# Splitting weight tiles into high and low halves: by ScalarE and GpSimd before, by two GpSimd-queue transfers after

## The chip, the cores and the metric

The kernel runs on one core of one Trainium2 chip. The metric is the device time of one execution in microseconds (us). Engines are named as the profile names them: PE is TensorE (PEld its weight loads), DVE is VectorE, ACT is ScalarE, POOL is GpSimd, SP is SyncE, which issues transfers.

## What is computed

One layer of a hybrid decoder (512 tokens, width 1024) and a final RMSNorm: a sparse-attention branch and a state-space (SSD) branch read one normalised input, are merged by gates and projected, and a gated feed-forward block with a short convolution follows.

```python
h = rmsnorm(x, norm_mix)
(q, c_raw, q_idx, k_idx, w_idx, z, xbc, dt_raw, g_att, g_ssm) = split_cols(h @ w_in, IN_SPLITS)
att = dsa_attention(...)                      # 16 heads, each query keeps 128 keys
y = gated_group_rmsnorm(ssd_scan(conv(xbc)) + d_skip * xs, z, ssm_norm)
merged = sigmoid(g_att) * (att @ w_att_out) + sigmoid(g_ssm) * (y @ w_ssm_out)
x = x + merged @ w_out
u = causal_depthwise_conv(rmsnorm(x, norm_ffn) @ w_ffn_up, conv_ffn_w, conv_ffn_b)
gate, val = split(u)
x = x + (silu(gate) * val) @ w_ffn_down
return rmsnorm(x, norm_final)
```

All of it is float32. TensorE multiplies here in a rounded form of float32 (`fp32r`), so every operand is kept as two tiles: `hi`, the value rounded, and `lo`, what the rounding left over. A product is the sum of three matmul passes, hi by hi, hi by lo and lo by hi (`mm3`).

## The kernel before

Weights come from HBM in tiles of 128 partitions by 1024 float32 (512 KB): 168 by `weight()` and two more (`load_kv`). Each goes through four steps in the kernel before: SP issues the load of `wr` (raw, 2 buffers, L95); ACT copies it with rounding to `wh` (3 buffers, `split`, L86); POOL subtracts, `wl = wr - wh` (3 buffers, L87); PE uses both, 24 matmuls of 512 columns a tile in most places. A tile's buffer comes free when its last reader is done.

The stages stand in this order: the first norm, the key indexer (`pqidx`), the SSD mixer (four groups; projections `pxbc`, `pz` and `pso` on PE woven into the scan; L331 to L333 pick the top keys), attention (`pq`, `pgs`, softmax on DVE and ACT, the bias tiles `bm` on POOL), the merge (`pga` with wG and `pao` with wAO, one tile each in turn), the output projection (`pwo`), the up projection (`pup`, 44 tiles of wUp, L105) and the down projection (`pdn`, 22 tiles of wDn, L947). In the mixer POOL has two small jobs for each chunk: the state `Hs` (L563, 8 of them) and the chunk's output `y` (L551, 12 of them). DVE works there on the decay tiles `dec` (L524, L527) and on the split of `X` (L508). A scheduler (the tile framework's) sets the order on every engine, and each engine takes its instructions strictly in that order: one that waits holds up all behind it.

Of the kernel before, what the change touches and what calls it, by code (L numbers as in the profile page):

```python
# [14 lines left out]
P = 128  # L15
# [33 lines left out]
def _body(ctx, tc, x, prm_d, cst_d, nfin_d, wI_d, wX_d, wSO_d, wQ_d, wG_d, wAO_d, wO_d, wUp_d, wDn_d,  # L49
# [34 lines left out]
    def split(hi, lo, src, lo_eng=None):  # L84
        """hi = fp32r(src), lo = fp32r(src - hi)."""
        nc.scalar.activation(hi, src, AF.Copy)  # L86
        (lo_eng or nc.vector).tensor_tensor(lo, src, f(hi), OP.subtract)  # L87

    wcnt = [0]

    def weight(src, w=1024):
        i = wcnt[0]
        wcnt[0] += 1
        raw = wp.tile([P, w], F32, tag="wr", name=f"wr{i}", bufs=2)
        nc.sync.dma_start(raw, src)  # L95
        hi = wp.tile([P, w], R32, tag="wh", name=f"wh{i}", bufs=3)
        lo = wp.tile([P, w], R32, tag="wl", name=f"wl{i}", bufs=3)
        split(hi, lo, raw, lo_eng=nc.gpsimd)
        return hi, lo

    def mm3(ps, terms):
        """ps = sum of lhs.T @ rhs over terms of ((lhs_hi, lhs_lo), (rhs_hi, rhs_lo))."""
        seq = [(a[0], b[0]) for a, b in terms] + [(a[0], b[1]) for a, b in terms] + [(a[1], b[0]) for a, b in terms]
        for i, (l, r) in enumerate(seq):
            nc.tensor.matmul(ps, l, r, start=(i == 0), stop=(i == len(seq) - 1))  # L105

    def rsqrt(dst, ss, scale, eps, n, pool):
        """dst = (ss*scale + eps)^-0.5"""
        t = pool.tile([P, n], F32, tag="rsq", name="rsq")
        nc.vector.tensor_scalar(t, ss, scale, eps, OP.mult, OP.add)  # L110
        nc.gpsimd.tensor_tensor(dst, t, mhalf[:, :n], OP.pow)
# [7 lines left out]
    def norm_T(xts, gname, dst, pool, sq, scl):  # L119
        """dst = rmsnorm(xts).T in hi and lo; sq and scl: the engine (ACT or DVE) of each block's squares and scaling."""  # L120
        for hf in range(2):
# [32 lines left out]

# [1 line left out]
    mid_stack = ExitStack()  # L156
# [18 lines left out]
    with tc.tile_pool(name="n1", bufs=2) as n1:  # L175
# [17 lines left out]

# [1 line left out]
        ps = mmt("pkidx")  # L195
# [37 lines left out]

# [1 line left out]
        dx = dtS.rearrange("p a b -> p (a b)")  # L235
# [39 lines left out]

# [1 line left out]
        pu = cht("pu")  # L277
# [4 lines left out]

# [1 line left out]
    nc.vector.tensor_copy(msk[:, 0:P], cv("maskc"))  # L284
# [3 lines left out]
    def dup_q(ps, name, tags, pool, scale, bufs):  # L288
        """Per head of a pair, its rows hi and lo on both halves of the partitions."""
        out = []  # L290
        for hh in range(2):
            r, o = slice(64 * hh, 64 * hh + 64), slice(64 - 64 * hh, 128 - 64 * hh)
            hi = pool.tile([P, S], R32, tag=tags[2 * hh], name=f"{name}h{hh}", bufs=bufs)
            lo = pool.tile([P, S], R32, tag=tags[2 * hh + 1], name=f"{name}l{hh}", bufs=bufs)
            nc.scalar.activation(hi[r], ps[r], AF.Copy, scale=scale)
            nc.vector.scalar_tensor_tensor(lo[r], ps[r], scale, f(hi[r]), OP.mult, OP.subtract)
            nc.sync.dma_start(f(hi[o]), f(hi[r]))
            nc.sync.dma_start(f(lo[o]), f(lo[r]))
            out.append((hi, lo))
        return out  # L300
# [39 lines left out]

# [1 line left out]
    def weave(chain, fill):  # L342
        """Emit the chain's (weight, step)s in order, the fillers spread between them by weight."""
        total = sum(w for w, _ in chain) or 1
# [11 lines left out]
    def proj_steps(name, wsrc, after, parts=2):  # L356
        """One column tile of a projection of actT, in emission steps."""
        st = {}
# [291 lines left out]

# [1 line left out]
    attT = []  # L652
# [11 lines left out]
    def load_kv():  # L664
        for i, nm in enumerate(("uk", "uv")):
            raw = wp.tile([P, 1024], F32, tag="wr", name="wr" + nm, bufs=2)
            nc.sync.dma_start(raw, wkv_d[i])
            hi = ap_.tile([P, 1024], R32, tag=nm + "h", name=nm + "h", bufs=1)
            lo = ap_.tile([P, 1024], R32, tag=nm + "l", name=nm + "l", bufs=1)
            split(hi, lo, raw, lo_eng=nc.gpsimd)  # L670
            wkv.append((hi, lo))
# [113 lines left out]
    def pav_(h):  # L785
        """Even heads: [Vh|Vl], odd heads: [Vl|Vh], so that the low part lands on the other half of the partitions."""
        p, hh = h // 2, h % 2
# [69 lines left out]

# [1 line left out]
    at.close()  # L859
# [19 lines left out]

# [1 line left out]
    x1 = [big.tile([P, D], F32, tag=f"ys{b}", name=f"x1{b}") for b in range(NB)]  # L881
# [124 lines left out]
def _coltile(w):  # L1006
    """(K, N) -> (N/128, 128, K/128 * 128): per column tile, rows on partitions."""
    k, n = w.shape
# [77 lines left out]
```

## Time and profile before

| | us |
|---|---|
| median of 3 runs | 1191.85 (1189.85 to 1192.34) |
| span of the profiled execution | 1188.0 |
| PE busy | 1113.1 (94%) |
| DVE busy | 705.9 (59%) |
| ACT busy | 582.3 (49%) |
| POOL busy | 518.0 (44%), of which L87 `wl`: 409.8 |

The profiled execution's time outside its span is not listed; the median of the runs lies 3.85 us above the span, and that is taken for it (its time is then 1191.85 us, the median itself). The page's part 1 gives the busy times, part 4 the chain that ended last: PE 57%, DVE 26%, ACT 5%, issue 3%, POOL 2%, DMA 2%.

### The profile page before, as it was taken

The page shows a single profiled execution, that of the slowest core. Times are in us where ns is not written, and L with a number is a line of the kernel's source. Part 1 is how long each engine was busy: PE and PEld are TensorE (multiplying, and loading weights), DVE is VectorE, ACT ScalarE, POOL GpSimd, SP SyncE. Part 2 cuts the span into 40 slices and gives each one's busy share as a digit, 9 for nine tenths or more (in the row PEclk, how much of TensorE's full clock was granted, in tenths as well). Part 3 has the DMA queues.
Part 4 walks back from the last instruction along what each step waited for, and adds up shares of the span by engine and source line. Part 5 has one row for each costly group of instructions (what it writes and reads, how often), then busy time and mean ns, then how long its engine had stood idle before and what let it go on. Part 6 is the DMA issues. An engine that isn't in the chain of part 4 may idle for free.

```text
span 1188.0 us, 14616 instructions
## 1 busy us (share of the span) xinstructions
PE 1113.1 (94%) x5268; PEld 920.8 (78%) x5268; DVE 705.9 (59%) x1324; ACT 582.3 (49%) x942; POOL 518.0 (44%) x287
## 2 busy tenths in 40 slices
PE   5898996998999889899999899999999999999997
PEld 5677775876887678778878788888888888888885
DVE  5569999998579689368988833305533344330004
ACT  5356464557476555456667633215444444432113
POOL 3324343334524434566566444444444444444442
PEclk9989999999999899999999999999999999999999
DMA  5264322222322231443434133232332222222221
GB/s 186 90 184 143 107 81 80 89 87 74 116 80 83 86 116 59 122 127 107 129 102 125 47 110 123 107 110 86 106 106 90 104 91 99 97 89 107 89 105 73
DMA packets 43306, 122.06 MB, mean 103 GB/s; under 512 B 5393, under 2 KB 9761, under 8 KB 43233
## 3 DMA queue, kind: packets, MB, share of 16 engines
q1 hardware_dynamic: 42656, 120.07, 30.5%
q8 instruction: 42, 0.69, 0.2%
q10 hardware_dynamic: 576, 1.05, 0.2%
q14 instruction: 32, 0.25, 0.1%
HBM read 108.29 MB, written 5.32 MB: 96 GB/s over the span
## 4 chain that ended last, share of the span: by engine, by line
PE 57%; DVE 26%; ACT 5%; issue 3%; POOL 2%; DMA 2%; POOLq 0%; DVEq 0%; ACTq 0%
PE pup L105 20%; PE pdn L947 10%; PE pso L464 5%; PE pao L105 4%; PE pga L105 4%; PE pwo L891 3%; DVE dec L524 3%; DVE u L388 3%; PE pxbc L373 3%; DVE msk L333 2%; DVE dec L527 2%; DVE m L332 2%; DVE pr L747 1%; DVE pr L759 1%; DVE Ml L87 1%
## 5 line engine op out<-in xcount | busy, mean ns | idle before, releaser
L87 POOL TENSOR_TENSOR wl<-wr,wh 128x1024 fp32r<-128x1024 f32 x168 | 409.8, 2440 | 481.4 <-ACT wh L86 260.6
L86 ACT ACTIVATE wh<-wr 128x1024 fp32r<-128x1024 f32 x168 | 177.4, 1057 | 189.1 <-PE pdn L947 80.6
L930 DVE SCALAR_TENSOR_TENSOR fu<-pup,prm,fu 128x511 f32<-128x511 f32 x88 | 65.9, 749 | 124.2 <-ACT fu L928 122.6
L105 PE MATMUL pup<-hTh,wh 128*128 128x512 f32 (+1 forms) x368 | 88.0, 381 | 1.6 <-ACT hTh L144 0.8
L105 PE MATMUL pup<-hTl,wh 128*128 128x512 f32 (+1 forms) x368 | 87.7, 380 | 0.0
L105 PE MATMUL pup<-hTh,wl 128*128 128x512 f32 (+1 forms) x368 | 87.5, 380 | 0.0
L105 PEld LDWEIGHTS pup<-hTh,wh 128*128 128x128 f32 x368 | 67.2, 188 | 15.1 <-ACT hTh L144 1.1
L105 PEld LDWEIGHTS pup<-hTl,wh 128*128 128x128 f32 x368 | 67.2, 188 | 13.1
L105 PEld LDWEIGHTS pup<-hTh,wl 128*128 128x128 f32 x368 | 67.2, 188 | 13.1
L947 PE MATMUL pdn<-wl,fh 128*128 128x512 f32 x176 | 68.6, 390 | 1.2 <-POOL wl L87 1.2
L947 PE MATMUL pdn<-wh,fl 128*128 128x512 f32 x176 | 68.5, 389 | 0.0
L947 PE MATMUL pdn<-wh,fh 128*128 128x512 f32 x176 | 68.4, 390 | 0.0
L974 DVE TENSOR_TENSOR x<-pdn,x 128x512 f32<-128x512 f32 x8 | 5.5, 690 | 104.6 <-PE pdn L947 104.6
L439 PE MATMUL pz<-wh,hTh 128*128 128x512 f32 x128 | 52.4, 409 | 9.9 <-DVE u L388 9.9
L388 DVE SCALAR_TENSOR_TENSOR u<-pxbc,prm,u 128x511 f32<-128x511 f32 (+2 forms) x72 | 53.2, 739 | 9.7 <-ACT u L386 9.3
L373 PE MATMUL pxbc<-hTh,wh 128*128 128x512 f32 x192 | 53.8, 413 | 4.1 <-ACT wh L86 2.9
L524 DVE TENSOR_SCALAR dec<-dec,acS 128x128 f32<-128x128 f32 x128 | 50.6, 450 | 8.9 <-DMA dec<-acD 8.9
L373 PE MATMUL pxbc<-hTh,wl 128*128 128x512 f32 x192 | 51.1, 393 | 0.0
L440 PE MATMUL pz<-wl,hTh 128*128 128x512 f32 x128 | 50.9, 398 | 0.0
L441 PE MATMUL pz<-wh,hTl 128*128 128x512 f32 x128 | 50.9, 398 | 0.0
L373 PE MATMUL pxbc<-hTl,wh 128*128 128x512 f32 x192 | 50.0, 391 | 0.0
L464 PE MATMUL pso<-yTh,wh 128*128 128x512 f32 x128 | 38.7, 426 | 11.4 <-ACT wh L86 7.9
(360 smaller groups left out, 2554.2 us busy)
## 6 DMA issues: line engine op xcount, KB each, us to landing
wr<-wUp SPq DMA_DIRECT2D x44, 512.0 KB, 3.4
wr<-wX SPq DMA_DIRECT2D x40, 512.0 KB, 3.5
wr<-wDn SPq DMA_DIRECT2D x22, 512.0 KB, 3.5
dec<-acD SPq DMA_DIRECT2D x32, 256.0 KB, 3.3
wr<-wSO SPq DMA_DIRECT2D x16, 512.0 KB, 3.5
wr<-wG SPq DMA_DIRECT2D x16, 512.0 KB, 3.6
x<-x SPq DMA_DIRECT2D x8, 512.0 KB, 4.9
wr<-wQ SPq DMA_DIRECT2D x8, 512.0 KB, 3.5
```

Source lines behind the costliest of these rows:

```text
L86: nc.scalar.activation(hi, src, AF.Copy)
L87: (lo_eng or nc.vector).tensor_tensor(lo, src, f(hi), OP.subtract)
L105: nc.tensor.matmul(ps, l, r, start=(i == 0), stop=(i == len(seq) - 1))
L373: nc.tensor.matmul(st["ps"], *st["it"][i], start=(i == 0), stop=(i == 23))
L388: nc.vector.scalar_tensor_tensor(u[:, d:], ps[:, :S - d], pv("cw", o + 3 - d, o + 4 - d), u[:, d:], OP.mult, OP.add)
L439: nc.tensor.matmul(ps, actT[k][0][:, bs], wh[:, ws], start=(k == 0), stop=False)
L440: nc.tensor.matmul(ps, actT[k][0][:, bs], wl[:, ws], start=False, stop=False)
L441: nc.tensor.matmul(ps, actT[k][1][:, bs], wh[:, ws], start=False, stop=(k == KD - 1))
L464: nc.tensor.matmul(ps, *seq[i], start=(i == 0), stop=(i == 11))
L524: nc.vector.tensor_scalar(dec[:, r, :], dec[:, r, :], acS[:, c, r0 + r:r0 + r + 1], 0.0, OP.subtract, OP.min)
L930: nc.vector.scalar_tensor_tensor(u[:, d:], ps[:, :S - d], pv("fw", o + 2 - d, o + 3 - d), u[:, d:], OP.mult, OP.add)
L947: nc.tensor.matmul(po8[b][hf], l[:, bs], r[:, ws], start=(k == 0 and i == 0), stop=(k == NF - 1 and i == 2))
```

## The change

`weight()` and `load_kv` no longer load a raw tile. `wsplit` issues a transfer from HBM straight into the `fp32r` tile `wh` on POOL's queue (the transfer converts), ACT writes `-wh` into `wl`, and a second transfer on POOL's queue reads the same weights from HBM again and adds them onto `wl`. The raw buffers are gone; `wh` and `wl` have 4 buffers each instead of 3. The matmuls are the same. (The diff also drops comments, which are left out here; lines after L86 move by some.)

```diff
+    def wsplit(hi, lo, src):
+        nc.gpsimd.dma_start(hi, src)
+        nc.scalar.activation(lo, f(hi), AF.Copy, scale=-1.0)
+        nc.gpsimd.dma_start(lo, src, accum_op=OP.add)
+
     def weight(src, w=1024):
         i = wcnt[0]
         wcnt[0] += 1
-        raw = wp.tile([P, w], F32, tag="wr", name=f"wr{i}", bufs=2)
-        nc.sync.dma_start(raw, src)
-        hi = wp.tile([P, w], R32, tag="wh", name=f"wh{i}", bufs=3)
-        lo = wp.tile([P, w], R32, tag="wl", name=f"wl{i}", bufs=3)
-        split(hi, lo, raw, lo_eng=nc.gpsimd)
+        hi = wp.tile([P, w], R32, tag="wh", name=f"wh{i}", bufs=4)
+        lo = wp.tile([P, w], R32, tag="wl", name=f"wl{i}", bufs=4)
+        wsplit(hi, lo, src)
         return hi, lo
@@ load_kv
-            raw = wp.tile([P, 1024], F32, tag="wr", name="wr" + nm, bufs=2)
-            nc.sync.dma_start(raw, wkv_d[i])
...
-            split(hi, lo, raw, lo_eng=nc.gpsimd)
+            wsplit(hi, lo, wkv_d[i])
```

POOL in the up projection, tiles 119 to 121 of wUp, the kernel before (`wr` raw, `wh` high, `wl` low; in brackets the semaphores it waits for):

```order
L87 TENSOR_TENSOR wl119_8034<-wr119_8031,wh119_8033 128x1024 [waits DMAHW0_49,PE_49,Activation_49]
L87 TENSOR_TENSOR wl120_8076<-wr120_8073,wh120_8075 128x1024 [waits DMAHW1_49,PE_49,Activation_49]
L87 TENSOR_TENSOR wl121_8110<-wr121_8107,wh121_8109 128x1024 [waits DMAHW2_49,PE_49,Activation_49]
```

The same place after, tiles 119 to 122:

```order
L93 DMA wh119_7910<-wUp 128x1024 [waits PE_49]
L95 DMA wl119_7911<-wUp 128x1024 [waits DMASW3_49,PE_49,Activation_49]
L93 DMA wh120_7951<-wUp 128x1024 [waits DMASW4_49,PE_49]
L93 DMA wh121_7984<-wUp 128x1024 [waits DMASW6_49,DMASW5_49,PE_49]
L95 DMA wl120_7952<-wUp 128x1024 [waits Activation_49]
L95 DMA wl121_7985<-wUp 128x1024 [waits DMASW0_49,DMASW7_49,PE_49,Activation_49]
L93 DMA wh122_8025<-wUp 128x1024 [waits PE_49]
L95 DMA wl122_8026<-wUp 128x1024 [waits DMASW1_49,PE_49,Activation_49]
```

One subtraction a tile has become two transfers, in a pattern of three tiles that repeats: one tile's pair alone, then two high transfers followed by their two low ones; each low one waits for ACT's negation of its own high tile.

POOL in the merge, tiles 88 to 91 (wG and wAO in turn), after:

```order
L93 DMA wh88_6665<-wG 128x1024 [waits PE_49]
L93 DMA wh89_6697<-wAO 128x1024 [waits DMASW6_49,DMASW5_49,PE_49]
L95 DMA wl88_6666<-wG 128x1024 [waits Activation_49]
L95 DMA wl89_6698<-wAO 128x1024 [waits DMASW7_49,Activation_49]
L93 DMA wh90_6733<-wG 128x1024 [waits DMASW0_49,PE_49]
L93 DMA wh91_6765<-wAO 128x1024 [waits DMASW1_49,PE_49]
```

Here the transfers go by pairs of tiles, with no lone tile between.

POOL in the mixer's second group, around the first states and outputs (`Hs1`, `y1_1`; `wr`, `wh`, `wl` are weight tiles), before:

```order
L563 TENSOR_TENSOR Hs1_2120<-Hs1_2120,cdec_113 128x512 [waits DVE_49]
L87 TENSOR_TENSOR wl29_2270<-wr29_2267,wh29_2269 128x1024 [waits DMAHW4_49,PE_49,Pool_49]
L551 TENSOR_TENSOR y1_1_2151<-y1_1_2151,t11_1_2240 128x512 [waits DVE_49]
L87 TENSOR_TENSOR wl30_2299<-wr30_2296,wh30_2298 128x1024 [waits DMAHW6_49,PE_49,Activation_49]
L87 TENSOR_TENSOR wl31_2422<-wr31_2419,wh31_2421 128x1024 [waits DMAHW1_49,PE_49,Activation_49]
L563 TENSOR_TENSOR Hs1_2120<-Hs1_2120,cdec_113 128x512 [waits DVE_49]
```

The same place after:

```order
L567 TENSOR_TENSOR Hs1_2092<-Hs1_2092,cdec_113 128x512 [waits DVE_49]
L95 DMA wl30_2267<-wX 128x1024 [waits DMASW5_49,PE_49,Activation_49]
L93 DMA wh31_2388<-wX 128x1024 [waits DMASW6_49,PE_49]
L555 TENSOR_TENSOR y1_1_2123<-y1_1_2123,t11_1_2211 128x512 [waits DVE_49,Pool_49]
L93 DMA wh32_2419<-wSO 128x1024 [waits DMASW7_49,DMASW0_49,PE_49]
L95 DMA wl31_2389<-wX 128x1024 [waits Activation_49]
L95 DMA wl32_2420<-wSO 128x1024 [waits DMASW1_49,DMASW2_49,PE_49,Activation_49]
L567 TENSOR_TENSOR Hs1_2092<-Hs1_2092,cdec_113 128x512 [waits DVE_49]
```

Where one subtraction stood between the state and `y1_1`, two transfers stand now, and three where two subtractions stood; each waits for a landing, for PE or for ACT.

## Rows read from the trace of the kernel before

**Rows 1.** The table by stretches: busy time and count per engine, clock, DMA.
```profile
core 0: us, PE busy (x) PEld busy (x) DVE busy (x) ACT busy (x) POOL busy (x), PEclk, DMA share, GB/s
...
80.00:480.00 400.00, 367.42 (x1753) 301.62 (x1752) 350.18 (x673) 234.99 (x351) 155.82 (x74) 0.96 0.28 95
...
530.00:680.00 150.00, 143.31 (x773) 120.71 (x772) 129.50 (x304) 102.02 (x242) 92.78 (x82) 0.99 0.36 102
680.00:821.00 141.00, 138.87 (x628) 113.54 (x627) 46.79 (x56) 45.15 (x63) 62.08 (x29) 1.00 0.31 110
821.00:1060.00 239.00, 239.00 (x1095) 199.53 (x1094) 99.23 (x136) 109.66 (x139) 103.86 (x44) 1.00 0.28 97
1060.00:1188.00 128.00, 119.76 (x527) 98.32 (x525) 14.84 (x28) 29.95 (x41) 49.81 (x24) 0.98 0.25 91
```

**Rows 2.** The chain that ended last, its tail: start us, length us, what.
```profile
758.54 5.46 PE pga L105 x24
764.00 5.60 PE pao L105 x24
...
820.94 238.70 PE pup L105 x1092
1059.65 103.37 PE pdn L947 x456
```

**Rows 3.** The timeline of one up-projection weight: start, length, engine, idle before.
```profile
890.84 1.98 PE L105 MATMUL pup<-hTh,wh 128*128 128x512 f32 x8
...
891.14 2.42 POOL L87 TENSOR_TENSOR wl<-wr,wh 128x1024 fp32r<-128x1024 f32 x1 [3.03 <-PE pup L105]
...
894.72 1.06 ACT L86 ACTIVATE wh<-wr 128x1024 fp32r<-128x1024 f32 x1 [0.60 <-PE pup L105]
...
896.28 1.98 PE L105 MATMUL pup<-hTh,wh 128*128 128x512 f32 x8
```

**Rows 4.** The timeline of the first norm, VectorE beside GpSimd.
```profile
14.45 0.75 DVE L137 TENSOR_SCALAR xngmix<-x,nrsgmix 128x1024 f32<-128x1024 f32 x1 [0.66 <-POOL nrsgmix L111]
...
15.86 2.34 POOL L87 TENSOR_TENSOR wl<-wr,wh 128x1024 fp32r<-128x1024 f32 x1
15.93 2.82 DVE L137 TENSOR_SCALAR xngmix<-x,nrsgmix 128x1024 f32<-128x1024 f32 x1 [0.67 <-POOL nrsgmix L111]
```

**Rows 5.** VectorE groups of the mixer: count | busy us, mean ns | idle before.
```profile
L524 DVE TENSOR_SCALAR dec<-dec,acS 128x128 f32<-128x128 f32 x128 | 50.6, 450 | 8.9 <-DMA dec<-acD 8.9
...
L527 DVE TENSOR_TENSOR dec<-dec,cb 128x512 f32<-128x512 f32 x32 | 27.5, 880 | 5.6 <-ACT dec L526 5.6
...
L508 DVE TENSOR_TENSOR X<-xdt,X 128x256 fp32r<-128x256 f32 x32 | 20.5, 674 | 0.0
```

**Rows 6.** The same lines by tile: min/median/max ns.
```profile
L524 DVE TENSOR_SCALAR dec<-dec,acS x128: 262/277/2501, 98.8 to 444.9; 128x128 f32<-128x128 f32 x128
L527 DVE TENSOR_TENSOR dec<-dec,cb x32: 669/681/2337, 128.1 to 447.9; 128x512 f32<-128x512 f32 x32
...
L508 DVE TENSOR_TENSOR X<-xdt,X x32: 401/416/2614, 131.7 to 470.0; 128x256 fp32r<-128x256 f32 x32
```

**Rows 7.** The page, part 6: a weight load, KB, us from issue to landing.
```profile
wr<-wUp SPq DMA_DIRECT2D x44, 512.0 KB, 3.4
```

**Rows 8.** The timeline, one issue on SP.
```profile
0.74 0.38 SPq L181 DMA_DIRECT2D x<-x  x1
```

**Rows 9.** Waits of GpSimd in the mixer: us in total, times, longest.
```profile
POOL Hs L563 <- DVE Hl L87: 35.6, 8, 10.5
POOL y L551 <- DVE t L550: 32.0, 7, 7.0
```

## The prediction

> **What bounds the kernel now.** I read the table by stretches first, then the chain, then one weight tile in the timeline. The table [rows 1] shows two kinds of stretch. From 680 us on PE is the bound: it is busy for 138.87 of 141 us, 239.00 of 239 and 119.76 of 128, and the chain [rows 2] is PE alone, 238.70 us of up projection and 103.37 us of down projection almost in one piece. The timeline [rows 3] shows why POOL does not matter there: the same step of the next tile begins on PE at 896.28 after 890.84, so a tile lasts 5.44 us, and in that time ACT spends 1.06 us and POOL 2.42 us on splitting one tile, both waiting for PE. In the merge two tiles take 5.46 and 5.60 us [rows 2], 11.06 a pair. In the mixer (80 to 480 us) PE is busy for 367.42 of 400 us and DVE for 350.18 [rows 1]: both are near full, and they wait for each other. Attention (530 to 680) is alike: PE 143.31 of 150, DVE 129.50.
>
> **What the change removes.** 168 subtractions on POOL and the two of `load_kv`, 2.4 us each [rows 3]. In the PE-bound stretches that is worth nothing. In the mixer it is worth something by way of DVE. The same DVE instruction, L137 on 128x1024, takes 0.75 us alone and 2.82 us when it starts 0.07 us after a POOL subtraction [rows 4]: it stands still until POOL is done. The mixer has the same pattern: L524 has a median of 277 ns, a maximum of 2501 and a mean of 450 [rows 5, 6]. Busy time over count times median gives what the stalls cost: L524 50.6 - 128 x 0.277 = 15.1 us; L527 27.5 - 32 x 0.681 = 5.7; L508 20.5 - 32 x 0.416 = 7.2; together 28.0 us. As PE's idle time in this stretch is 32.6 us, the most that can be won is about that; I take 22, three quarters of the stall, since PE has work of its own for 367 us and what DVE gives back then meets it. SP loses 170 loads and the waits before them; what that frees is the decay tiles' load, for which DVE waited 8.9 us [rows 5], and this too lies within PE's 32.6. ACT does one copy a tile as before, 1.06 us: nothing.
>
> **What it adds: the price of a tile.** Per tile there are two transfers where there was one. Between 821 and 1060 us the transfers are nearly all weights, and they moved 97 GB/s at a share of 0.28 of the 16 DMA engines [rows 1], so 346 GB/s when all are at work, and 512 KB take 1.5 us. The high transfer is at least this copy: h = 1.5, no less; if the conversion halves the rate, 3.0; I take 1.5, the row of the same bytes from the same place. The accumulating transfer has to read the tile that it adds to besides the source. No row shows one. Its ends are 1.5 us (the second read is hidden) and 4.5 (two reads and a write one after the other); I take two reads, l = 3.0. It cannot be below zero, since the single load that both replace was hidden. The Trainium skill prices this in "Collectives: The Full Stack", section "The bandwidth ceiling": an add in the DMA engine costs its second read and nothing else, 62.28 GB/s for a copy against 32.35 for a reduction; by that estimate l would be 2.9 and the sum some 7 us lower. No run here shows it.
>
> **The cycle in POOL's queue.** POOL takes its queue in order, and in the up and down projections it repeats every three tiles: a high and its low transfer, then two high and their two low. A low one cannot be issued before its high one has landed and ACT has negated it, and everything behind waits with it; all of it goes through one queue, so a later transfer's bytes come behind the earlier ones. Landing takes 3.4 us from issue [rows 7], of which 1.5 is moving and about 0.4 the issue (SP's own takes 0.38 [rows 8]): 1.5 us from the last byte to the signal. Then ACT, 1.1, and the issue of the low transfer. What an issue costs on POOL no row shows: 0.38 us as on SP [rows 8], up to the 2.42 of the subtraction that it replaces [rows 3]; I take 0.5, near the row that is also an issue. So the DMA engines stand idle for 1.5 + 1.1 + 0.5 = 3.1 us behind the lone high transfer, and 3.1 - 1.5 = 1.6 us behind the pair, whose second transfer fills part of it. A cycle of three tiles takes 3 x (1.5 + 3.0) + 3.1 + 1.6 = 18.2 us. PE needs 3 x 5.44 = 16.3. PE, which never waited for weights here, then waits 1.9 us in every cycle. With 44 tiles of up and 22 of down projection, 22 cycles: **+42 us**. The fourth buffer covers the first few tiles; I leave that to the range. The point where it turns is h + l = (16.3 - 4.7) / 3 = 3.9 us a tile. The skill's "DMA: Bandwidth & Descriptors", section "Specifications", gives about 1 us to the first byte on GpSimd's path against 0.6 on SP's; by that estimate each cycle would lose 0.8 us more and the sum would be 18 us higher. No run here shows that either.
>
> **The other stretches.** In the merge the order is by pairs, 2 x 4.5 + 1.6 = 10.6 us against PE's 11.06: 0, with +30 at l = 4.5 (13.6 us, 12 pairs). In the mixer there are 51 tiles in 400 us, 7.8 us each, so the queue has room on average, but the 8 `Hs` and 12 `y` jobs of POOL now stand behind transfers that wait for a round trip of 3.4 + 1.1 + 0.5 = 5.0 us. Their cover is that POOL waits for their operands now, 35.6 and 32.0 us [rows 9], 3.4 us a job. What is left over, 1.6 us on 20 jobs, is 32 us if every job is hit and 0 if none; I take a third, +10, because DVE's next steps wait for these jobs. The mixer's net is -12. In attention the `bm` tiles on POOL lose as much to the same queue as DVE gains from fewer stalls: 0, between -7 (PE's idle time there) and +7.
>
> **The sum.** The profiled execution's time is its span of 1188.0 and the 3.85 around it, 1191.85, which is the median. 1191.85 - 12 + 42 = **1222 us**.
>
> **Rival one: the transfers keep up.** If h + l is under 3.9 us, say l = 1.5, a cycle takes 13.7 us, PE stays the bound from 680 us on, and the kernel keeps the 22 us of the mixer and some 5 of attention: 1165 us, at best 1152 with all of PE's idle time in both. For it speaks that DMA engines are at 0.28 to 0.36 in most stretches [rows 1]; against it, that a share does not tell the wait of a queue that goes in order.
>
> **Rival two: the transfers are slow.** With l = 4.5 a cycle takes 22.7 us: 22 x 6.4 = +141, the merge +30, and the mixer, at 7.6 us a tile against 7.8, loses its gain and the 10 us: 1191.85 + 181 = 1373 us. A conversion at half rate does the same. For it speaks that nothing in the trace adds or converts in a transfer, and that each microsecond on a tile costs 66 in the last two stages alone; against it, that plain bytes move at 346 GB/s.
>
> If the converting transfer did not round and only copied, the low half would be nothing but the same two transfers would run: no other time.
>
> **Chances.** Forecast case (h + l of 4 to 5.3 us, 1190 to 1300 us): 0.42. Rival one: 0.30. Rival two: 0.28. A measurement of this kernel tells about 0.2% from no change, 1189.5 to 1194.2 us; 0.03 falls there from the edges of the first two cases, so faster 0.29, slower 0.68. Of rival one a third lies below 1150, of rival two a third above 1400; so the range is 1150 to 1400. The forecast's own range is 1190 to 1300.
>
> **What would show it.** Between 821 us and the end PE should have gaps that end with a low tile's landing, one a cycle, and the up projection's piece of the chain should be near 270 us for 238.70. DVE's L524 should fall from 450 to below 300 ns a piece, and the time from 80 us to the query projections should be shorter by some 10 us. A low transfer should take about twice the engine time of a high one. The forecast is wrong if the up projection stays at 239 us (rival one), or goes beyond 300 (rival two).

## The result, and the profile after

The changed kernel takes **1286.14 us** (median; 1276.61 to 1291.41) against 1190.85 for the kernel before (1187.06 to 1192.34): ratio 1.0809, 95% interval 1.0751 to 1.0868. The profiled execution is the shortest of its runs, 1276.61 us with a span of 1274.8, so 1.8 us lie around the span. (It is 1.7 to 2.1 us in the runs of every kernel, so the profiled execution of the kernel before is the one of 1189.85 us, and the 3.85 taken ahead of the prediction is some 2 us too much.) The runs of the changed kernel differ by TensorE's granted clock: 0.966 of full speed in the shortest, 0.952 to 0.954 in those of 1291.3 and 1291.4.

To see where the time went, I cut both traces at the same events: the first matmul of `pxbc` (mixer), `pq` (attention), `pga` (merge), `pup` and `pdn`.

| stretch, us | before | after | measured | forecast |
|---|---|---|---|---|
| start | 76.1 | 79.0 | +2.9 | 0 |
| mixer | 402.7 | 402.1 | -0.6 | -12 |
| attention | 200.4 | 208.0 | +7.6 | 0 |
| merge, output projection | 137.3 | 150.9 | +13.6 | 0 |
| up projection | 243.0 | 270.6 | +27.6 | +28 |
| down projection, end | 128.5 | 164.3 | +35.8 | +14 |
| span | 1188.0 | 1274.8 | +86.8 | +30 |

(The forecast's +42 for both projections is divided by tiles, 44 and 22.)

The page of the changed kernel, parts 1, 3, 4 and 6: busy time, the queue that carries the weights, the chain that ended last, and issues (KB, median us from issue to landing).

```profile
PE 1134.6 (89%) x5268; PEld 927.3 (73%) x5268; DVE 617.0 (48%) x1324; ACT 572.5 (45%) x942; POOL 348.7 (27%) x457
...
q0 software_dynamic: 48960, 178.28, 61.0%
...
PE 31%; issue 23%; DMA 20%; DVE 11%; ACT 8%; POOL 6%; POOLq 0%; ACTq 0%; DVEq 0%; SPq 0%
DMA wh<-wUp 6%; PE pao L109 4%; PE pga L109 3%; DMA dec<-acD 3%; PE pup L109 3%; DMA wh<-wDn 3%; ACT wl L94 3%; PE pso L468 3%; PE pxbc L377 3%; POOL wh L93 3%; POOL wl L95 2%; PE pq L377 2%; DVE u L392 2%; DMA wh<-wX 2%; PE pwo L893 2%
...
wh<-wUp POOLq DMA_DIRECT2D x44, 512.0 KB, 6.8
...
dec<-acD SPq DMA_DIRECT2D x32, 256.0 KB, 5.6
```

PE was 57% of the chain and is 31% now; transfers and issue, 5% together before, are 43%. Of PE, DVE, ACT and POOL none is busier than it was, apart from PE by two percent (its clock, below): this is time spent waiting.

The same five stretches in the table by stretches (mixer, attention, merge, up, down), to hold against [rows 1], and behind them the first 60 us of the up projection alone:

```profile
core 0: us, PE busy (x) PEld busy (x) DVE busy (x) ACT busy (x) POOL busy (x), PEclk, DMA share, GB/s
79.00:481.00 402.00, 369.05 (x1768) 302.83 (x1767) 303.56 (x678) 238.34 (x358) 103.52 (x126) 0.97 0.69 161
481.00:689.00 208.00, 190.12 (x976) 159.01 (x976) 136.12 (x347) 123.12 (x275) 99.59 (x123) 0.97 0.72 166
689.00:840.00 151.00, 140.66 (x620) 113.71 (x618) 32.08 (x54) 43.24 (x62) 36.70 (x52) 0.99 0.75 179
840.00:1110.00 270.00, 249.71 (x1102) 203.75 (x1103) 94.84 (x136) 99.41 (x136) 60.55 (x86) 0.97 0.70 164
1110.00:1274.00 164.00, 131.86 (x532) 103.53 (x530) 17.18 (x32) 33.62 (x46) 30.94 (x44) 0.93 0.62 150
...
840.00:900.00 60.00, 60.00 (x310) 51.67 (x311) 23.36 (x37) 25.23 (x38) 13.59 (x20) 1.00 0.73 166
```

In the up projection PE was busy for all of 239.00 us; now it stands still for 20.3 of 270, and its 1102 matmuls take 249.71 us where 1095 took 239.00: the clock is 0.97 instead of 1.00. In the down projection idle time rises from 8.2 to 32.1 us and the same work from 119.76 to 131.86 us, at 0.93. The timeline of PE shows where the lower clock begins (start, length, what, idle time before):

```profile
986.17 3.62 PE L109 MATMUL pup<-hTh,wl 128*128 128x512 f32 x8 [2.61 <-DMA wl<-wUp]
...
1024.34 2.11 PE L109 MATMUL pup<-hTh,wl 128*128 128x512 f32 x8 [2.63 <-DMA wl<-wUp]
```

Eight matmuls take 1.98 us [rows 3]. Behind a wait of 2.61 us they take 3.62, nearly the double: most of them ran at the lower of the clock's two levels, 1.2 GHz for 2.4 (the granted clock is 0.57 from 986 to 990 us). Behind another wait of 2.63 us they take 2.11 (1.00 from 1024 to 1028). Of the ten waits for low tiles in this stage four, of 2.04 to 2.71 us, are followed by 3.1 to 3.6 us, and six, of 0.75 to 2.63, by 2.1. So the clock falls behind some of these waits and not behind others that are as long; what decides it, no run shows.

POOL's queue in the up and the down projection of the changed kernel (L93 high, L95 low):

```profile
964.00 0.88 POOL L93 DMA_DIRECT2D wh<-wUp  x1
972.08 0.85 POOL L95 DMA_DIRECT2D wl<-wUp  x1 [7.20 <-ACT wl L94]
972.62 1.42 POOL L93 DMA_DIRECT2D wh<-wUp  x2
980.62 0.88 POOL L95 DMA_DIRECT2D wl<-wUp  x1 [6.58 <-ACT wl L94]
982.23 0.87 POOL L95 DMA_DIRECT2D wl<-wUp  x1 [0.74 <-ACT wl L94]
982.78 0.88 POOL L93 DMA_DIRECT2D wh<-wUp  x1
...
1118.60 0.88 POOL L93 DMA_DIRECT2D wh<-wDn  x1
1126.53 0.85 POOL L95 DMA_DIRECT2D wl<-wDn  x1 [7.05 <-ACT wl L94]
1127.07 0.87 POOL L93 DMA_DIRECT2D wh<-wDn  x1
```

Read it by what stands between two high transfers. In the up projection a lone tile lasts from 964.00 to 972.62, 8.6 us, for 5.44 of PE's [rows 3]; a pair from 972.62 to 982.78, 10.2 us, for 10.9 of PE's. The whole cycle of three is 18.8 us. So a pair keeps up and a lone tile does not. This is one cycle; the twelve between 869.01 and 1099.06 us take 19.2 on average, a lone tile 8.2 to 9.3 us and a pair 9.8 to 11.2. In the down projection three lone tiles follow each other, the first of them shown: 8.5, 8.3 and 8.2 us. Over the whole stage a lone tile takes 8.1 to 10.7 us.

What POOL's transfers wait for in the up projection (860 to 1080 us), and the high ones of the down projection (1110 to 1260): us in total, times, longest.

```profile
POOL wl L95 <- ACT wl L94: 168.3, 34, 7.9
POOL wh L93 <- PE pup L109: 2.2, 1, 2.2
...
POOL wh L93 <- PE pdn L949: 0.6, 1, 0.6
```

The high transfers hardly ever wait for PE: the queue sets the pace, and PE follows it. The time that PE loses to its lower clock therefore comes, for the most part, out of time in which it would otherwise wait.

In the mixer most of the DVE stalls are gone and the stretch is no shorter. The group L528 of DVE there (count | busy, mean ns | idle before), which was L524 in [rows 5]:

```profile
L528 DVE TENSOR_SCALAR dec<-dec,acS 128x128 f32<-128x128 f32 x128 | 32.5, 311 | 32.4 <-DMA dec<-acD 32.3
```

The mean fell from 450 to 311 ns, DVE's busy time in the mixer from 350 to 304 us; but the wait for the decay tiles' loads rose from 8.9 to 32.3 us. ACT's and DVE's timelines show a second new wait:

```profile
318.14 1.06 ACT L94 ACTIVATE wl<-wh 128x1024 fp32r<-128x1024 f32 x1 [5.39 <-DMA wh<-wX]
319.11 1.13 ACT L86 ACTIVATE Mh<-dec 128x512 fp32r<-128x512 f32 x2
320.15 0.71 ACT L511 ACTIVATE X<-xdt 128x256 fp32r<-128x256 f32 x2
...
320.58 0.76 DVE L512 TENSOR_TENSOR X<-xdt,X 128x256 fp32r<-128x256 f32 x2 [4.88 <-ACT X L511]
```

ACT stands 5.39 us before the negation until a high tile has landed; `Mh` and `X` are queued behind it and go at once when it is done, and DVE has waited 4.88 us for that `X`.

### The profile page after: what moved, and what is told of

It reads as the page before. It is cut to its first block, busy times and chain, and to the rows that moved or that the text cites. A ratio compares the mean times of both kernels' runs of the same rounds, so it can differ in the third digit from the quotient of the medians.

```text
span 1274.8 us, 14670 instructions
## 1 busy us (share of the span) xinstructions
PE 1134.6 (89%) x5268; PEld 927.3 (73%) x5268; DVE 617.0 (48%) x1324; ACT 572.5 (45%) x942; POOL 348.7 (27%) x457
## 4 chain that ended last, share of the span: by engine, by line
PE 31%; issue 23%; DMA 20%; DVE 11%; ACT 8%; POOL 6%; POOLq 0%; ACTq 0%; DVEq 0%; SPq 0%
DMA wh<-wUp 6%; PE pao L109 4%; PE pga L109 3%; DMA dec<-acD 3%; PE pup L109 3%; DMA wh<-wDn 3%; ACT wl L94 3%; PE pso L468 3%; PE pxbc L377 3%; POOL wh L93 3%; POOL wl L95 2%; PE pq L377 2%; DVE u L392 2%; DMA wh<-wX 2%; PE pwo L893 2%
## 5 line engine op out<-in xcount | busy, mean ns | idle before, releaser
L94 ACT ACTIVATE wl<-wh 128x1024 fp32r<-128x1024 f32 x168 | 177.3, 1057 | 459.6 <-DMA wh<-wUp 139.3
L109 PE MATMUL pup<-hTh,wl 128*128 128x512 f32 (+1 forms) x368 | 94.3, 401 | 20.1 <-DMA wl<-wUp 20.1
L109 PEld LDWEIGHTS pup<-hTh,wl 128*128 128x128 f32 x368 | 69.5, 197 | 38.8 <-DMA wl<-wUp 25.3
L95 POOL DMA_DIRECT2D wl<-wUp x44 | 38.2, 868 | 209.8 <-ACT wl L94 205.1
L949 PE MATMUL pdn<-wl,fh 128*128 128x512 f32 x176 | 72.8, 414 | 20.6 <-DMA wl<-wDn 20.6
L95 POOL DMA_DIRECT2D wl<-wX x40 | 35.7, 893 | 189.2 <-ACT wl L94 175.4
L949 PE MATMUL pdn<-wh,fh 128*128 128x512 f32 x176 | 71.5, 409 | 3.7 <-DVE fu L932 3.6
L949 PE MATMUL pdn<-wh,fl 128*128 128x512 f32 x176 | 71.3, 405 | 0.0
L949 PEld LDWEIGHTS pdn<-wl,fh 128*128 128x128 f32 x176 | 34.7, 197 | 32.7 <-DMA wl<-wDn 25.5
L87 DVE TENSOR_TENSOR fl<-fu,fh 128x512 fp32r<-128x512 f32 x22 | 15.2, 692 | 78.1 <-ACT fh L86 78.1
L95 POOL DMA_DIRECT2D wl<-wDn x22 | 19.0, 863 | 117.9 <-ACT wl L94 108.6
```

What stands on the lines that cost most here:

```text
L94: nc.scalar.activation(lo, f(hi), AF.Copy, scale=-1.0)
L95: nc.gpsimd.dma_start(lo, src, accum_op=OP.add)
L949: nc.tensor.matmul(po8[b][hf], l[:, bs], r[:, ws], start=(k == 0 and i == 0), stop=(k == NF - 1 and i == 2))
```

## The experiments

The stretches of each kernel's profiled execution, cut as above, us (each experiment's ratio, below, is to the kernel before as it was timed beside it, hence the range in the first row):

| kernel | start | mixer | attention | merge | up | down | time, median |
|---|---|---|---|---|---|---|---|
| before | 76.1 | 402.7 | 200.4 | 137.3 | 243.0 | 128.5 | 1188.57 to 1190.85 |
| changed | 79.0 | 402.1 | 208.0 | 150.9 | 270.6 | 164.3 | 1286.14 |
| e1, no subtraction | 61.9 | 365.7 | 188.0 | 138.7 | 244.9 | 128.1 | 1130.4 |
| e2, plain low | 77.9 | 379.2 | 199.4 | 140.3 | 241.6 | 134.8 | 1174.32 |
| e3, early preset | 84.0 | 381.5 | 192.8 | 138.0 | 244.9 | 130.9 | 1167.82 |
| e4, high by SP and ACT | 69.5 | 394.6 | 205.0 | 142.0 | 245.6 | 132.3 | 1191.75 |
| e5, four pieces | 71.5 | 395.0 | 198.5 | 138.0 | 246.1 | 128.2 | 1177.63 |
| e6, eight pieces | 70.1 | 389.8 | 204.1 | 139.0 | 246.5 | 128.4 | 1178.84 |
| e7, POOL waits | 82.6 | 388.2 | 209.8 | 180.7 | 315.7 | 185.3 | 1369.75 |
| e8, ACT waits | 81.3 | 396.0 | 204.1 | 138.1 | 246.7 | 128.5 | 1197.49 |
| e9, one ahead | 81.4 | 403.4 | 204.2 | 140.4 | 247.4 | 132.1 | 1213.11 |
| e10, two ahead | 84.7 | 417.4 | 201.3 | 155.0 | 246.8 | 162.0 | 1273.37 |
| e11, early and plain | 79.7 | 371.6 | 191.6 | 138.0 | 243.7 | 127.0 | 1153.31 |
| e12, eight pieces in the mixer | 72.0 | 388.9 | 198.9 | 137.2 | 244.0 | 128.5 | 1171.59 |
| e13, halves | 71.1 | 396.6 | 196.7 | 137.5 | 243.0 | 128.8 | 1177.33 |
| e14, fixed low tile | 62.7 | 365.9 | 188.8 | 138.7 | 246.1 | 128.2 | 1132.61 |

**What the subtraction costs (e1, e14).** Edit of the kernel before:

```diff
+    zl = const.tile([P, 1024], R32, tag="zl", name="zl")
+    nc.vector.memset(f(zl), 0.0)
...
-        lo = wp.tile([P, w], R32, tag="wl", name=f"wl{i}", bufs=3)
-        split(hi, lo, raw, lo_eng=nc.gpsimd)
-        return hi, lo
+        nc.scalar.activation(hi, raw, AF.Copy)
+        return hi, zl
```

> The kernel before, with POOL's subtraction left out: every low weight tile is one fixed tile of zeros, so the products hi by lo use zeros. Loads, ACT's copies and the matmuls are as before. It prices what the subtraction costs in the mixer by way of DVE's stalls, with no new transfers. The prediction's term (22 us of DVE stalls come back as time): 1170 us, 80 us to the first query projection shorter by 20 us or more, and attention by a few. The rival (PE paces the mixer and the stalls were in its shadow): within 5 us of the kernel before, 1186 to 1192, although DVE is busy some 45 us less in the mixer.

Measured: 1130.4 us, ratio 0.9505 (0.9476 to 0.9534). The mixer is 37.0 us shorter, the start 14.2, attention 12.4. The mixer in the table by stretches, the kernel before above and e1 below:

```profile
76.00:479.00 403.00, 370.42 (x1767) 304.18 (x1766) 350.86 (x674) 235.97 (x352) 158.22 (x75) 0.96 0.28 96
...
62.00:428.00 366.00, 358.49 (x1767) 297.73 (x1766) 303.91 (x677) 237.72 (x355) 28.79 (x23) 1.00 0.34 105
```

The gain is larger than PE's idle time of 32.6 us [rows 1]: idle is 7.5 us now, and the matmuls themselves take 358.49 us for 370.42 over as many of them before, at a clock of 1.00 for 0.96. So the subtraction did hold the mixer up, by more than the forecast took. DVE is busy for 47 us less, but POOL's `Hs` and `y` no longer stand behind subtractions either, and e1 does not tell the two apart. The low tile of e1 is all zeros; e14 fills it with small numbers instead, to tell whether the zeros gave the clock.

> The kernel before with the subtraction left out, as in the first run, but the fixed low tile that all products hi by lo use holds small numbers (weights of the first up tile times 2 to the -12) instead of zeros. If the 58 us that leaving it out gave come from DVE's and POOL's time, nothing changes: 1128 to 1136 us, mixer 363 to 369. If zeros in a third of the matmuls were what kept TensorE's clock up (0.996 of the span against 0.98), the clock falls and the time is 1140 or more.

Measured: 1132.61 us (0.9525, 0.9491 to 0.9559), clock 0.996 of the span as in e1. It is not the zeros.

**Bytes or round trip (e2, e3).** In `wsplit`, e2 above, e3 below:

```diff
-        nc.gpsimd.dma_start(lo, src, accum_op=OP.add)
+        nc.gpsimd.dma_start(lo, src)
...
-        nc.scalar.activation(lo, f(hi), AF.Copy, scale=-1.0)
+        nc.scalar.activation(lo, mhalf[:, 0:1].to_broadcast([P, lo.shape[1]]), AF.Copy, scale=0.0)
```

> The changed kernel with the low transfer as a plain converting copy onto wl (no addition; the low half is then the high half again). It still waits for ACT's negation of its own high tile, the queue's order is the same, and only the transfer's second read is gone. Theory (bytes and round trip add up in a cycle): 3 x 1.2 us less of 18.8, so 15.2 us a cycle, below PE's 16.3: up projection back at 240 to 245 us, down near 105, total about 1205. Rival one (the round trip alone sets the cycle): up stays 265 to 270, total 1270 or more. Where the mixer's missing gain is put down to the load on the DMA engines, the wait of DVE for the decay tiles falls from 32.3 us to below 15 and the mixer is 5 to 10 us shorter.

> The changed kernel with the low tile preset to zero instead of to the negated high half (ACT writes the same 1.06 us, but needs no landing of the high tile); the low transfer then adds the weights onto zero, so the low half is the weights themselves and nothing is subtracted. All bytes, both transfers and the addition are the same; what is gone is the wait of the low transfer for its high one. Theory (bytes and round trip add up): the cycle falls to 3 x 4.0 = 12 us, below PE's 16.3: up projection 239 to 245 us, total about 1195 to 1205. Rival two (bytes on the DMA engines alone set the pace): up stays at 265 to 270, total 1270 or more.

Measured: 1174.32 (0.9871, 0.9836 to 0.9906) and 1167.82 us (0.9811, 0.9775 to 0.9848). Either edit alone gives the up projection back, 241.6 and 244.9 us, so neither the bytes nor the round trip costs it alone: they add up in the queue's cycle, and each rival falls. Both totals lie some 30 us below what was expected of them (1205, and 1195 to 1205), since the mixer, attention and the merge got shorter too, by 42 us together in e2 and 49 in e3. e2 also gives the prices. Its page says of the weights' queue:

```profile
q0 software_dynamic: 48960, 178.28, 49.4%
```

and the page of e4 (below), where that queue carries the accumulating transfers and only two plain ones:

```profile
q0 software_dynamic: 24768, 90.19, 45.1%
```

49.4% of 1173.2 us over 340 plain transfers is 1.70 us of the 16 engines each; 61.0% of 1274.8 over the changed kernel's 340 is 2.29, so an accumulating one took 2 x 2.29 - 1.70 = 2.87 us (with the high ones as in e2), 1.7 times a plain one. In e4 it is 45.1% of 1189.0 us over 172 transfers, less the two plain ones: 3.13 us, 1.8 times. (The Trainium skill, "Collectives: The Full Stack", section "The bandwidth ceiling", has an add cost its second read alone, a ratio of 1.93 between its two rates. The ratio here, 1.7 to 1.8, is a little lower.) In e2 DVE's wait for the decay tiles did not fall below 15 us, as I had expected, but to 20.9.

**Half of the change (e4).**

```diff
...
-        wsplit(hi, lo, src)
+        nc.sync.dma_start(raw, src)
...
+        nc.scalar.activation(hi, raw, AF.Copy)
+        nc.scalar.activation(lo, f(hi), AF.Copy, scale=-1.0)
+        nc.gpsimd.dma_start(lo, src, accum_op=OP.add)
```

> Half of the change: the high half is made as in the kernel before (SP loads the raw tile, ACT rounds it; 2 raw, 3 high and 3 low buffers), then ACT negates it onto wl and the accumulating transfer on POOL's queue adds the weights from HBM, as in the changed kernel. One transfer a tile is left on POOL's queue, and it waits for ACT alone, not for a landing; ACT has one more 1.06 us a tile. Theory (the round trip in POOL's queue is what costs after the merge): up projection back at 239 to 245 us and down near 105; with the subtraction off POOL the whole is at or below the kernel before, 1175 to 1195 us. Rival (accumulating transfers alone are too slow): up stays above 260 and the total above 1250.

Measured: 1191.75 us (1.0023, 1.0005 to 1.0042). With one transfer on POOL's queue that waits for no landing, up takes 245.6 and down 132.3 us. The accumulating transfers are not too slow; the pair in one queue was. The mixer is 8 us shorter than before, of the 37 that the missing subtraction is worth.

**Which queue's wait takes the mixer's gain (e7, e8).** Both start from e3; e7 above, e8 below:

```diff
+        nc.gpsimd.tensor_copy(lo[:, 0:1], f(hi)[:, 0:1])
...
+        nc.scalar.activation(wscr, f(hi)[:, 0:1], AF.Copy)
```

> The run with the early preset, with one wait put back on POOL alone: ACT presets the low tile to zero without waiting for the high one, and POOL casts one column of the high tile into the low one between the two transfers, so that POOL's queue stands until the high tile has landed, as in the changed kernel, and ACT does not (the low half is again wrong: the weights themselves are added onto zero). Theory A (in the mixer the time goes into ACT's wait for landings, 36.4 us there, and what stands behind it on ACT): the mixer stays near the early preset's 381.5 us, up to 388, while the up projection goes back to 255 to 270 us, since there the queue's round trip counts. Theory B (the mixer's time goes into POOL's queue, where the states and outputs stand behind the waiting transfers): mixer 395 to 403 us.

> The run with the early preset, with the wait put back on ACT alone: ACT presets the low tile to zero, and a second ACT instruction of one column reads the high tile into a scratch column, so that ACT's queue stands until the landing as in the changed kernel; the two transfers on POOL do not wait for each other (the low half is wrong as in the early preset). Theory A (ACT's wait for landings is what takes the mixer's gain): mixer 395 to 403 us, up projection below 250 us. Theory B (POOL's queue): mixer 380 to 388 us, up projection below 250.

Measured: 1369.75 us (1.1518, 1.1471 to 1.1564) and 1197.49 (1.0070, 1.0048 to 1.0091). In the mixer POOL's wait costs 388.2 - 381.5 = 6.7 us and ACT's 396.0 - 381.5 = 14.5. That speaks for theory A in the larger part and leaves some room for B. Neither figure is exact. The executions of e3 alone lie 9 us apart, and the profiled one is its slowest, so 6.7 us do not stand clear of that. And e8's second ACT instruction takes 203 ns a tile, some 10 us for the mixer's 51 tiles, so that its 14.5 us are wait and instruction together; the changed kernel, which has both waits and not this instruction, lies 13.9 us above e7. After the merge it is the other way round: ACT's wait costs nothing (up 246.7, down 128.5), and POOL's costs more than I had expected, since nearly every tile is a lone one in e7, as POOL's timeline there shows:

```profile
965.20 0.87 POOL L93 DMA_DIRECT2D wh<-wUp  x1
972.06 0.18 POOL L95 CAST wl<-wh 128x1 fp32r<-128x1 f32 x1 [6.00 <-DMA wh<-wUp]
972.54 0.86 POOL L96 DMA_DIRECT2D wl<-wUp  x1 [0.30 <-POOL wl L95]
973.26 0.70 POOL L93 DMA_DIRECT2D wh<-wUp  x1
```

From 965.20 to 973.26 is 8.1 us; the mean of the 28 tiles from 881.28 to 1093.10 us is 7.6, for 5.44 of PE's.

**The last part of the mixer (e11).** Both edits, of e2 and e3, together:

> The changed kernel with neither of the two costs: the low tile is preset without the high one's landing (as in the early preset) and the low transfer is a plain converting copy (as in the plain low), so the low half is the weights themselves. Two transfers a tile are left, with no second read and no wait between them. It tells what of the mixer's 16 us, which the early preset (381.5 us) still has over the kernel without subtraction (365.7), is the second read. Theory (the load of the accumulating transfers makes the decay tiles late for DVE: that wait is 36.0 us in the early preset, 11.2 without subtraction): the wait falls to 10 to 18 us and the mixer to 364 to 372 us; total 1140 to 1160. Rival (the 16 us are POOL's work of issuing and its order): mixer 376 to 384 us, total 1160 to 1172.

Measured: 1153.31 us (0.9695, 0.9677 to 0.9714), mixer 371.6. So of the 15.8 us between e1 and e3 the second read is 9.9 and the two plain transfers are 5.9. DVE's wait for the decay tiles is 21.7 us, for 36.0 in e3 and 11.2 in e1: it follows the load, less than I had expected. Late landing is not all of it: in e2 the decay tiles land 3.7 us after issue (median of the kernel) as in e1, and DVE waits 20.9 us for them. The rival, POOL's work of issuing, was not tested by itself.

**The order in the queue (e9, e10).** The changed kernel; each high transfer is issued ahead of the low one of an earlier tile, and an ordering edge holds it there:

```diff
...
+        while len(high) < min(i + 2, len(SEQ)):
+            m, t = SEQ[len(high)]
+            high.append(wp.tile([P, w], R32, tag="wh", name=f"wh{len(high)}", bufs=4))
+            hins.append(nc.gpsimd.dma_start(high[-1], wd[m][t]))
+        hi = high[i]
...
+        tc.add_manual_dep(low.ins, hins[-1].ins.name, mybir.DependencyInfo(mybir.DependencyClass.NoSync, mybir.DependencyReason.DATA), reason="order")
```

(`SEQ` lists the 168 tiles in their order; e10 has `i + 3`.)

> The changed kernel complete, with only the order of transfers on POOL's queue changed: each high transfer is issued one tile ahead, so that the queue alternates high of tile i+1, low of tile i, all the way (before: a lone pair, then two high and two low). The same bytes, the same ACT work, the same 4 + 4 buffers. A low transfer's high one then has one tile's time (5.4 us on PE) more to land, of the 6.7 + 1.1 us that it needs. Theory A (the round trip in the in-order queue, not the bytes, is what costs after the mixer): up projection 243 to 250 us, down 128 to 133, merge 137 to 142; in the mixer ACT waits less for landings and the stretch falls from 402 to 380 to 392 us; total 1165 to 1185 us, below the kernel before. Rival (bytes and engine time set the pace): up stays above 260 us and the total above 1250.

> The same with each high transfer issued two tiles ahead of its low one, which then finds it landed and negated. Theory A: up and down as in the run with one tile ahead (240 to 250 and 128 to 133 us); ACT's wait for landings in the mixer falls from 36.4 us to below 10 and the mixer is 375 to 390 us; total 1160 to 1185. Against it: a low transfer now stands behind a high one that waits for a buffer which comes free two tiles earlier at most, so where the queue is the limit the last tiles of a stage come later. Rival: above 1250 us.

Measured: e9 1213.11 us (1.0184, 1.0153 to 1.0216), e10 1273.37 (1.0712, 1.0683 to 1.0742). After attention e9 confirms theory A with nothing left out of the computation: merge 140.4, up 247.4, down 132.1 us, together 66 us less than in the changed kernel, by order alone. POOL's timeline and PE's busy time there:

```profile
972.12 0.55 POOL L113 DMA_DIRECT2D wh<-wUp  x1 [3.27 <-PE pup L125]
973.10 0.86 POOL L117 DMA_DIRECT2D wl<-wUp  x1 [0.43 <-ACT wl L116]
977.56 0.55 POOL L113 DMA_DIRECT2D wh<-wUp  x1 [3.60 <-PE pup L125]
979.17 0.86 POOL L117 DMA_DIRECT2D wl<-wUp  x1 [1.06 <-ACT wl L116]
```

```profile
829.00:1077.00 248.00, 243.81 (x1113) 204.06 (x1114) 99.46 (x142) 107.24 (x144) 62.37 (x89) 0.99 0.89 190
```

The high transfers come every 5.44 us, PE's own time, and wait for PE; the low ones wait about 1 us or less. The DMA share is higher than in the changed kernel (0.89 for 0.70), and PE runs: the bytes alone are not the limit. In the mixer both miss: 403.4 and 417.4 us, and so do both totals. ACT still waits there for landings (38 us in e9), and the high transfers now wait for PE to free their buffers (160 us in e9, 22 in the changed kernel) ahead of POOL's own jobs; which of the two takes the time is not shown. With two ahead a low transfer also stands behind a high one that waits for a buffer, and PE waits for the low tile, as the waits of e10's last stretches show:

```profile
PE pdn L965 <- DMA wl<-wDn: 24.8, 18, 2.6
```

**Another way to spare DVE (e5, e6, e12, e13).** The kernel before, with POOL's subtraction in pieces:

```diff
-        split(hi, lo, raw, lo_eng=nc.gpsimd)
+        nc.scalar.activation(hi, raw, AF.Copy)
+        for a in range(0, w, 256):
+            nc.gpsimd.tensor_tensor(lo[:, a:a + 256], raw[:, a:a + 256], f(hi)[:, a:a + 256], OP.subtract)
```

> The kernel before with POOL's subtraction cut into four pieces of 256 columns; no transfer is changed. Leaving the subtraction out was worth 58 us (1188.89 to 1130.4), 37 of them in the mixer (402.7 to 365.8 us). Theory (a DVE instruction that meets a POOL one stands still until that one instruction ends): a stall is then about a quarter as long, 0.6 us for 2.4, DVE's L524 falls from a mean of 450 ns to below 360, and half or more of the 58 us comes back: 1150 to 1165 us. Rival (DVE loses the time that POOL is busy, however it is cut): 1180 to 1195 us.

> The same with eight pieces of 128 columns. Theory (the stall is the rest of one POOL instruction): as four pieces or up to 8 us better, 1145 to 1165 us, unless the fixed time of a POOL instruction makes POOL late (eight pieces over 4 us a tile): then worse than four pieces. Rival (busy time counts, not the cut): 1180 to 1200 us.

Measured: 1177.63 us (0.9900, 0.9879 to 0.9921) and 1178.84 (0.9911, 0.9877 to 0.9944). Some gain, a fifth of e1's: both times lie far above what the theory expected and a little below the rival's range, so neither holds as it was put. The group of DVE's L526 (L524 before), and POOL's pieces by tile (min/median/max ns), in e5:

```profile
L526 DVE TENSOR_SCALAR dec<-dec,acS 128x128 f32<-128x128 f32 x128 | 48.2, 430 | 11.2 <-DMA dec<-acD 11.2
```

```profile
L100 POOL TENSOR_TENSOR wl<-wr,wh x672: 717/741/1716, 9.6 to 1156.0; 128x256 fp32r<-128x256 f32 x168
```

The mean of DVE's instruction fell to 430 ns only (391 with eight pieces), and not below 360 as expected, and four pieces take 4 x 0.74 = 3.0 us for 2.4. (The Trainium skill, "SBUF — State Buffer", section "Terms", has the port pair of DVE and GpSimd held for a full instruction, with the loser standing still. [rows 4] agree; that shorter instructions would therefore stall DVE much less is what I had made of it, and e5 does not bear it out.)

> The kernel before with the subtraction cut into eight pieces of 128 columns in the first 58 tiles only (start and mixer), whole in the others. Adding the stretches of the runs: start 70.1 and mixer 389.8 us as with eight pieces everywhere, the rest as before (200.4 + 137.3 + 243.0 + 128.5): 1169 us for the span, 1165 to 1177 for the time. Rival (the stretches do not add, since the order in attention changes with them): 1178 to 1190.

> As the run with eight pieces in the first 58 tiles, but of these every second tile gets its low half as in the run with SP's raw load and one accumulating transfer (ACT negates the high half, POOL's queue adds the weights). DVE's stalls, ACT's extra copies and the load of the transfers are all halved. If waits grow faster than load, the mixer is shorter than with either alone (389.8 and 394.6 us): 378 to 388, total 1155 to 1168 us. If the costs only mix: 390 to 394 and 1168 to 1180.

e12 keeps the cut to the tiles of start and mixer: 1171.59 us (0.9868, 0.9849 to 0.9887), within its forecast. It is 1.3% faster than the kernel before. e13 takes e4's way for every second of these tiles: 1177.33 us (0.9910, 0.9894 to 0.9927). The two costs do not shrink faster than their loads: the mixer, 396.6 us, is no shorter than with either alone.

## Why the prediction was right, and where wrong

**Direction and the queue's mechanism were right; the order, and the mixer's terms, were not.** The time is longer, for the larger part by the cycle in POOL's queue. PE's gaps end with a low tile's landing, as the prediction said they would; PE's waits of the changed kernel from 840 us to the end (us in total, times, longest):

```profile
PE pdn L949 <- DMA wl<-wDn: 20.6, 10, 2.8
PE pup L109 <- DMA wl<-wUp: 20.1, 10, 2.7
```

In the up projection they come from 928 us on, one a cycle as forecast. Each ends with the first low tile of a pair, which was issued behind the lone tile: the wait at 986.17 us ends with the transfer issued at 980.62. So the lone tile delays the one behind it. Point by point:

- Price of a tile: h = 1.5 and l = 3.0 were forecast, 1.70 and 2.87 measured (3.13 by e4), 4.6 to 4.8 in sum for 4.5. The sum did not come down to the break-even of 3.9 that rival one needed, and rival two's l = 4.5 was far off. A low transfer takes 1.7 to 1.8 times a high one, for "about twice".
- Cycle of three tiles: 18.2 us forecast, 19.2 measured on average; up projection +28 forecast, +27.6 measured, 270.6 us for "near 270" (the stretch; the chain's own pieces of PE are far shorter now). That the two agree so closely is luck: 44 tiles at 19.2 us for three would take 281 us, but PE runs without a wait from 840 to 900 us on tiles that are there already, a cover that the forecast left to the range. (The Trainium skill, "DMA: Bandwidth & Descriptors", section "Specifications": by its first-byte times each cycle would have been an estimated 0.8 us longer. The cycle is 1.0 longer than forecast, but POOL's issue of 0.85 to 0.88 us, taken as 0.5, explains most of that, and no run here tells the two apart.)
- **The step that failed first is the order.** "In the up and down projections it repeats every three tiles", and in the merge "the order is by pairs": I read this from the rows of eight tiles, none of them of the down projection. Counted through the whole order, the merge and output projection have 8 lone tiles and 8 pairs, the up projection 14 and 15, the down projection 10 and 6. With the forecast's own prices (a lone tile 4.5 + 3.1 = 7.6 us, a pair 10.6) this gives 145.6 us for 24 tiles that PE does in 132.7 (5.53 each [rows 2]): +13. Up: 265.4 - 239.4 = +26. Down: 139.6 - 119.7 = +20, where 14 was forecast. Counting alone would have made +59 of the +42. That order is the cause e9 shows: 66 of the 77 us that the three stretches lost come back with the same bytes.
- **The merge and the output projection: +13.6 where 0 was forecast.** That the count gives +13 is chance, for the merge itself lost nothing: from 690 to 780 us PE is busy for 89.52 us of 90, since the high transfers wait there for PE. The loss lies behind it, in the output projection's tiles and in the second norm, whose steps on POOL (`nrsgffn`, L115) stand among the transfers in the same queue (the one at 832.04 us follows a low transfer that had waited 6.1 us for ACT). PE's waits from 690 to 840 us:

```profile
PE pwo L893 <- DMA wl<-wO: 5.3, 3, 2.3
PE nTgffn L143 <- DVE xngffn L141: 4.3, 3, 2.8
```

In this stretch PE's idle time is up by 9.6 us, and its busy time by 4, in part at a lower clock (0.99). The forecast had no term for the second norm.

- **Down, the remaining 16 us.** The ten lone tiles take 9.0 us each on average, not 7.6, and the six pairs 9.9: together some 150 us for 139.6. Why a lone tile takes longer than 4.5 + 3.1 us is not taken apart, and some 6 us, at the stage's start and end, stay open. PE's work takes 12 us longer at a clock of 0.93, but that is no further cost where the queue sets the pace. e9 shows that it is the order: the same bytes, 132.1 us.
- **The mixer's gain was mis-sized, and so was its cost.** The prediction took 22 us and at most PE's idle 32.6: the subtraction is worth 37.0 us there (e1). Idle time was no upper bound, since PE's own work gets 12 us shorter when it no longer has to wait. (DVE's L528 came down to 311 ns with the change, not below 300.) The gain in the start (14) and in attention (12) I left out or set against the `bm` tiles.
- The cost in the mixer was put at 10 us, POOL's `Hs` and `y` behind waiting transfers. That one is 6.7 us (e7). Missing were two others. "ACT does one copy a tile as before, 1.06 us: nothing" is the sentence that failed: the copy is the same, but in the mixer it waits 15 times, 36.4 us, for the landing of a wX tile, where the raw tile's load, issued early, was nearly always done (the kernel before has three such waits for wSO, 10.5 us, and none for wX); and all of ACT's mixer work is queued behind it: some 14 us (e8, with its own extra instruction; 13.9 by e7 and the changed kernel). And the transfers' load: two plain ones 5.9 us, the second read 9.9 (e11). The decay tiles land 5.6 us after issue for 3.3 before, and DVE waits longer for them, but that this is the whole way by which the load costs time is argued and not shown.

The mixer's account, each step with its run:

| | us |
|---|---|
| mixer before | 402.7 |
| no subtraction on POOL (e1) | -37.0 |
| two plain transfers a tile (e11 - e1) | +5.9 |
| the second read (e3 - e11) | +9.9 |
| POOL's queue waits for the landing (e7 - e3) | +6.7 |
| ACT's queue waits for it (e8 - e3) | +14.5 |
| sum | 402.7 |
| measured | 402.1 |

Each entry comes from one profiled execution of each kernel, and executions of one kernel differ by several us, so that the sum meets the measurement within 1 us is chance. The 37.0 and the 14.5 stand clear of that; which of the three small terms is the largest does not. Part of each is order too, since the scheduler places instructions a little differently in each kernel, and the terms need not add.

In attention the +7.6 us follow the same pattern (e1 188.0, e3 192.8, e2 199.4, changed 208.0), and its cause stays open. PE has one long wait there that the kernel before has not, 7.7 us at 521 us for `kT`'s load; but e2, faster than the kernel before in this stretch, has it too (9.5 us). The last 9.5 us between the profiled execution and the median come with lower granted clocks; why the clock differs from run to run, and whether it is the cause, stays open.

## What to carry to other kernels

An in-order queue that issues both a transfer and one that depends on its landing pays a round trip for each, unless something else stands between: here about 9 us for a lone tile and 10 for two, and reordering alone gave 66 us back after attention (and nothing in the mixer). Count the whole order of such a queue before taking a pattern from a few rows, and look at every engine that the dependence runs through: an instruction of the same length and count on ACT cost some 14 us because of what it now waited for. Where GpSimd and DVE share a stretch, price GpSimd's work by a run without it, and keep a remedy to the stretch that needs it, as e12 does.

## What the runs showed of the hardware

- An accumulating transfer to SBUF of 512 KB takes 2.9 to 3.1 us of the 16 DMA engines (the changed kernel, e4), a plain converting one 1.70 (e2); POOL is busy 0.55 to 0.88 us with issuing one.
- Behind some waits TensorE works at its lower clock: eight matmuls of 1.98 us took 3.62 us behind a wait of 2.61 us, and 2.11 behind one of 2.63. Over the up projection nearly the same number of matmuls took 10 us longer, in the mixer with a quarter of the idle time (e1) 12 us less.
- GpSimd's subtraction, 410 us of POOL's busy time in all (the table of times ahead of the prediction), costs 58 us of the kernel's time with DVE near full in the mixer; cutting it into pieces of a quarter gave back a fifth of that.
